# One transformer layer on one core: the feed-forward's next operands built two small steps per block instead of a pair of tiles at three places

## The chip, the cores and the metric

The kernel runs on one core of one Trainium2 chip. The metric is the time on the device in microseconds (us), a median over runs. A profile is one execution, taken by the hardware profiler. The engines are TensorE (PE; its weight loads are PEld), VectorE (DVE), ScalarE (ACT), GpSimd (POOL) and SyncE (SP). All DMAs of this kernel are issued from SP's queue, in the order in which they stand there.

## The reference, cut to what matters

One layer over 2048 latent tokens and 128 context tokens of width 1024: attention and a short convolution, an output projection, then a feed-forward network of hidden width 2816. The change lies in the feed-forward part, which works on all 2176 tokens:

```python
x = x + gate_a * rms_norm(mix, g_attn_post)
u = rms_norm(x, g_ffn_pre) * (1.0 + scale_f) + shift_f
gu = u @ w_ffn_in
h = jax.nn.silu(gu[..., :D_FF]) * gu[..., D_FF:]
return x + gate_f * rms_norm(h @ w_ffn_out, g_ffn_post)
```

Everything is float32.

## The kernel before, in words

**Stages.** Input projections, attention with the convolution and the output projection interleaved, then the feed-forward's up-projection (`u @ w_ffn_in`), then its down-projection. After the output projection each of the 17 tiles of 128 tokens (0 to 15 latent, 16 context) lies in DRAM as `x2d[ti]`, with its inverse norm in a column of `r2s`.

**Precision.** A float32 matrix is split into a high part, a cast by ScalarE (line 82), and the remainder, a subtraction by VectorE (line 83); `split` does both. A product is then three matmuls: high times high, high times low, low times high.

**The up-projection** uses Strassen's scheme in Winograd's form: the four quadrants of the weights of one block and the four quadrants of the operand `u` give seven combinations each, and seven products instead of eight. Columns of weights come in `NF` = 22 blocks (index `f`), tokens in three chunks (index `c`) of 5, 6 and 6 tiles. Two tiles form a pair: their quadrants b11 and b21 come from the first tile, b12 and b22 from the second. A single tile (the fifth of chunk 0) is halved instead. The matmuls are 320 columns wide in chunk 0 and 384 in chunks 1 and 2.

**One block** (`up_unit`, lines 948 to 992) is 7 products x 4 slices x 3 matmuls = 84 matmuls, lines 956, 957 and 959, into four PSUM banks called a, b, c and d (two buffers each, so all of PSUM). VectorE and ScalarE combine the banks (lines 965 to 984), POOL multiplies the second hidden half (line 986), and SP stores both halves. Beside it `wi_ops` (line 913) makes the next block's seven weight operands: POOL forms four sums `st` (line 918), then come seven splits into `wi`. The raw weights come by two loads of 512 KB a block, into the tag `t4`, which has four buffers.

**Building the operand.** The seven combinations of `u` for a pair of tiles come from `build_pair`, which calls `build_tile` for each tile: load the row `x2d[ti]` (512 KB, again a buffer of `t4`), scale it on POOL (line 835), then twice: four transposes on TensorE into one PSUM bank (line 841) and four scalings by VectorE into `ur` (line 842). Then come seven outputs; four of them need a subtraction on POOL first (line 859, tile `td`, two buffers). Chunk 0's are kept in SBUF (`build_kept`, during the output projections). Those of chunks 1 and 2 are built while the chunk before runs (`build_spilled`): each output is split into `hl`, which has one buffer, and stored to DRAM (512 KB to `u2d`). Their transposes use bank d. The operands come back by `u_load` from block 19 on.

**Order.** The program is written as one sequence, and each engine gets its own queue, drawn up when the program is built (`schedule_with_timeline_sim=True`): of what is ready on a simulated timeline, what was written earlier goes first. An engine then executes its queue in that order. So instructions of a build, written after block 2, stand among those of blocks 3 to 6 in each queue.

## Time and profile before

| | us |
|---|---|
| median of 3 runs | 3112.84 |
| lowest and highest | 3108.48, 3118.28 |
| the profiled execution | 3102.96 |
| its span, first to last instruction | 3101.2 |
| up-projection: first and last matmul start | 1570.7, 2574.5 |

The span is counted on the engines; the execution's time has a little more around it. Busy shares of the span: PE 94%, PEld 86%, DVE 67%, ACT 44%, POOL 42%. In the rows below, `L82` is line 82 of the kernel before; `out<-in` gives the tiles written and read; `x48` is a count; a bracket at a row's end holds the idle time of the engine before that instruction, and what ended it. Rows of one line and one tile give the shortest, median and longest duration in ns, then the first and last start in us. Rows of waits give the total in us, the number of times and the longest. Matmul ends are modelled by the profiler, so stretches of time are taken from one matmul's start to another's.

### The profile page before, as it was taken

The page shows a single profiled execution, that of the slowest core. Times are in us where ns is not written, and L with a number is a line of the kernel's source. Part 1 is how long each engine was busy: PE and PEld are TensorE (multiplying, and loading weights), DVE is VectorE, ACT ScalarE, POOL GpSimd, SP SyncE. Part 2 cuts the span into 40 slices and gives each one's busy share as a digit, 9 for nine tenths or more (in the row PEclk, how much of TensorE's full clock was granted, in tenths as well). Part 3 has the DMA queues.
Part 4 walks back from the last instruction along what each step waited for, and adds up shares of the span by engine and source line. Part 5 has one row for each costly group of instructions (what it writes and reads, how often), then busy time and mean ns, then how long its engine had stood idle before and what let it go on. Part 6 is the DMA issues. An engine that isn't in the chain of part 4 may idle for free.

```text
span 3101.2 us, 47350 instructions
## 1 busy us (share of the span) xinstructions
PE 2926.7 (94%) x16921; PEld 2661.2 (86%) x16921; DVE 2080.6 (67%) x4116; ACT 1370.9 (44%) x2425; POOL 1296.4 (42%) x1135
## 2 busy tenths in 40 slices
PE   4789989999999999999999999999999999999998
PEld 3567879999999999988888888999899998788886
DVE  7996547887887887764467775676655554554443
ACT  3433225665655665663444343333333333443333
POOL 7653115554554554542246554554544540111110
PEclk8899999999999999999999999999999999999999
DMA  6776473463464354347635565434643235666663
GB/s 248 234 227 218 154 244 112 120 213 107 120 191 125 109 177 129 110 152 228 203 129 161 154 192 192 155 129 147 216 156 101 96 103 187 237 227 217 219 217 121
DMA packets 351180, 525.26 MB, mean 169 GB/s; under 512 B 33088, under 2 KB 264672, under 8 KB 349152
## 3 DMA queue, kind: packets, MB, share of 16 engines
q1 hardware_dynamic: 350944, 522.23, 52.7%
q8 instruction: 133, 2.18, 0.3%
q14 instruction: 103, 0.84, 0.1%
HBM read 393.79 MB, written 128.34 MB: 168 GB/s over the span
## 4 chain that ended last, share of the span: by engine, by line
PE 65%; DVE 14%; DMA 8%; issue 7%; POOL 4%; ACT 2%; SPq 0%; POOLq 0%; DVEq 0%; ACTq 0%
PE psg L956 7%; PE psg L959 6%; PE psg L957 6%; PE s L502 6%; PE psy L1087 4%; PE psy L1085 4%; PE psy L1086 4%; PE t L546 3%; DVE wi L83 2%; DMA raw<-in_w_fi 2%; PE psx L725 2%; PE psx L726 2%; PE psx L724 2%; PE o L539 2%; DMA u2d<-hl 2%
## 5 line engine op out<-in xcount | busy, mean ns | idle before, releaser
L956 PE MATMUL psg<-u,wi 128*128 128x384 f32 (+1 forms) x1848 | 617.4, 335 | 42.6 <-ACT wi L82 18.0
L957 PE MATMUL psg<-u,wi 128*128 128x384 f32 (+1 forms) x1848 | 607.3, 329 | 0.0
L959 PE MATMUL psg<-u,wi 128*128 128x384 f32 (+1 forms) x1848 | 591.5, 331 | 4.5 <-DVE wi L83 4.5
L505 DVE TENSOR_SCALAR_CACHE_REDUCE e<-s 128x436 f32<-128x436 f32 (+2 forms) x648 | 373.4, 600 | 87.0 <-PE s L502 71.4
L956 PEld LDWEIGHTS psg<-u,wi 128*128 128x128 f32 x1848 | 351.6, 190 | 61.7 <-ACT wi L82 27.6
L959 PEld LDWEIGHTS psg<-u,wi 128*128 128x128 f32 x1848 | 348.5, 190 | 9.0 <-DVE wi L83 8.5
L502 PE MATMUL s<-km,qt 128*128 128x436 f32 (+1 forms) x1280 | 344.4, 372 | 10.8 <-DVE e L505 8.5
L957 PEld LDWEIGHTS psg<-u,wi 128*128 128x128 f32 x1848 | 352.0, 190 | 0.1
L83 DVE TENSOR_TENSOR wo<-rawo,wo 128x1024 fp32r<-128x1024 f32 x132 | 167.0, 1265 | 248.6 <-ACT wo L82 243.9
L83 DVE TENSOR_TENSOR wi<-st,wi 128x512 fp32r<-128x512 f32 x264 | 234.4, 892 | 131.3 <-ACT wi L82 129.7
L510 ACT ACTIVATE e<-e,nm 128x2176 f32<-128x2176 f32 (+1 forms) x136 | 273.9, 2014 | 76.9 <-DVE nm L509 76.2
L82 ACT CAST wi<-st 128x512 fp32r<-128x512 f32 x264 | 163.0, 620 | 324.1 <-POOL st L918 161.4
L1087 PE MATMUL psy<-wo,hhl 128*128 128x512 f32 x748 | 285.5, 390 | 1.8 <-DVE hhl L83 1.8
L1086 PE MATMUL psy<-wo,hhl 128*128 128x512 f32 x748 | 285.9, 390 | 0.9 <-DVE wo L83 0.9
L1085 PE MATMUL psy<-wo,hhl 128*128 128x512 f32 x748 | 285.6, 390 | 0.0
L82 ACT CAST wo<-rawo 128x1024 fp32r<-128x1024 f32 x132 | 139.1, 1054 | 297.7 <-PE psy L1087 288.6
L502 PEld LDWEIGHTS s<-km,qt 128*128 128x128 f32 x1280 | 209.4, 190 | 23.6 <-DVE e L505 16.3
L83 DVE TENSOR_TENSOR atl<-t,ath 128x512 fp32r<-128x512 f32 (+2 forms) x292 | 187.2, 650 | 34.2 <-ACT ath L82 33.6
L82 ACT CAST ath<-t 128x512 fp32r<-128x512 f32 (+2 forms) x292 | 157.3, 555 | 113.6 <-PE t L546 111.1
L1058 POOL TENSOR_TENSOR rr<-rr,mhalf 128x1 f32<-128x1 f32 x17 | 13.1, 779 | 450.2 <-DVE rr L1057 450.2
L918 POOL TENSOR_TENSOR st<-raw,st 128x512 f32<-128x512 f32 x66 | 103.4, 1566 | 229.7 <-DVE wi L83 229.7
L238 PE MATMUL pq<-wh,uh 128*128 128x512 f32 x408 | 172.4, 433 | 19.9 <-DVE t L297 15.2
(264 smaller groups left out, 7183.9 us busy)
## 6 DMA issues: line engine op xcount, KB each, us to landing
raw<-in_w_fi SPq DMA_DIRECT2D x132, 512.0 KB, 4.1
rawo<-in_w_fo SPq DMA_DIRECT2D x132, 512.0 KB, 3.5
fu<-ud SPq DMA_DIRECT2D x256, 256.0 KB, 4.7
raw<-in_w_ada SPq DMA_DIRECT2D x48, 512.0 KB, 4.8
u2d<-hl SPq DMA_DIRECT2D x42, 512.0 KB, 3.8
u<-u2d SPq DMA_DIRECT2D x14, 1536.0 KB, 9.5
hr<-hid SPq DMA_DIRECT2D x110, 192.0 KB, 3.5
hid<-hid SPq DMA_DIRECT2D x88, 192.0 KB, 1.9
```

What stands on the lines that cost most here:

```text
L82: S.copy(h, src)
L83: (eng or V).tensor_tensor(l, src, h.bitcast(F32), op=ALU.subtract)
L238: T.matmul(pq, u[kt][0][:, sl], wh[j, kt], start=(kt == 0), stop=False)
L502: mm = T.matmul(ps[:, :n], qt[:, s, m, t * P:(t + 1) * P], km[m][:, k0:k0 + n], start=(s == 0), stop=(s == 1))
L505: V.tensor_scalar(et[:, k0:k0 + n], ps[:, :n], SCALE, None, op0=ALU.mult, op1=ALU.max, accum_out=mx[:, ci:ci + 1])
L510: S.activation(et[:, :nk], et[:, :nk], AF.Exp, bias=nm, scale=1.0, accum_out=sm[:, t, m:m + 1])
L956: T.matmul(ps[:, :n], h[:, ks], u[:, 0, kt, :n], start=start and kt == 0, stop=False, skip_group_check=not start)
L957: T.matmul(ps[:, :n], h[:, ks], u[:, 1, kt, :n], start=False, stop=False, skip_group_check=not start)
L959: T.matmul(ps[:, :n], l[:, ks], u[:, 0, kt, :n], start=False, stop=stop and kt == 3, skip_group_check=not start)
L1085: T.matmul(banks[i][:, b, :], hh, woh_[:, bs], start=(f == 0), stop=False)
L1086: T.matmul(banks[i][:, b, :], hh, wol_[:, bs], start=False, stop=False)
L1087: T.matmul(banks[i][:, b, :], hl, woh_[:, bs], start=False, stop=(f == NF - 1))
```

## The change

`build_tile` and `build_pair` become generators, cut into steps. A tile has two steps of four transposes and four scalings (the first also has the row's load and its scaling on POOL); each of the seven outputs is a step, with its subtraction where it has one. A pair is 11 steps, a chunk 33. Before, a whole pair was written after blocks 2, 8 and 14 of the chunk that runs; now one step is written after block 0 and two after each of blocks 1 to 18, so that the 33 end with block 16. The outputs come in the order 2, 1, 3, 4, 0, 5, 6 instead of 0, 5, 6, 2, 1, 3, 4, for chunk 0's kept operands also. Nothing else differs: the same instructions on the same tiles and buffers.

```diff
@@ build_tile
+            yield ur
-        return ur
@@ build_pair
+        us = []
+        for ti in pair:
+            for ur in build_tile(ti, bank):
+                yield
+            us.append(ur)
         if len(pair) == 2:
-            ua, ub_ = (build_tile(ti, bank) for ti in pair)
+            ua, ub_ = us
...
-        out(0, w, b11)
-        out(5, w, b21)
-        out(6, w, b22)
         t = diff(b12, b11)
         out(2, w, t)
+        yield
         t2_ = diff(b22, t)
         out(1, w, t2_)
+        yield
         out(3, w, diff(t2_, b21))
+        yield
         out(4, w, diff(b22, b12))
+        yield
+        for i, src in ((0, b11), (5, b21), (6, b22)):
+            out(i, w, src)
+            yield
@@ build_kept
-        build_pair(chunks[0][k], pst_bank, out)
+        for _ in build_pair(chunks[0][k], pst_bank, out):
+            pass
@@ build_spilled
-    def build_spilled(c, k):
+    def build_spilled(c):
+        for i in range(7):
+            u2d[c, i] = dram.tile([P, 2, 4, widths[c]], F32, name=f"u2d{c}{i}")
+        for k, pair in enumerate(chunks[c]):
...
+            yield from build_pair(pair, lambda: bank("d"), out)
@@ for c in range(3): for f in range(NF):
-            if c < 2 and f % 6 == 2 and f // 6 < 3:
...
-                build_spilled(c + 1, f // 6)
+            if c < 2 and f < NF - 3:
+                steps = build_spilled(c + 1) if f == 0 else steps
+                for _ in range(2 if f else 1):
+                    next(steps, None)
```

## The prediction, made before the changed kernel ran

> **What bounds the kernel now.** I read the page first, then the feed-forward stage block by block. The page gives TensorE nearly the whole span and the largest share of the chain that ended last; the last row here is the stage that the change touches.

> ```profile
> span 3101.2 us, 47350 instructions
> PE 2926.7 (94%) x16921; PEld 2661.2 (86%) x16921; DVE 2080.6 (67%) x4116; ACT 1370.9 (44%) x2425; POOL 1296.4 (42%) x1135
> PE 65%; DVE 14%; DMA 8%; issue 7%; POOL 4%; ACT 2%; SPq 0%; POOLq 0%; DVEq 0%; ACTq 0%
> ...
> L956 PE MATMUL psg<-u,wi x1848: 302/334/657, 1570.7 to 2574.2; 128*128 128x384 f32 x125, 128*128 128x320 f32 x60
> ```

> The change lies in the up-projection, from 1570.7 us on, three chunks of 22 blocks. A block is 84 matmuls of lines 956 to 959 (seven products of four triples), so every 84th of them in the timeline marks a block's start. The busy times by stretch follow; after the two times stand its length, the engines' busy times, the granted clock, DMA share and GB/s. First chunk 0 without its first block and chunk 1 without its first two, then an undisturbed block of each width (320 and 384 columns).

> ```profile
> 1589.54:1890.39 300.85, 280.86 (x1813) 270.42 (x1813) 233.18 (x342) 122.39 (x232) 181.47 (x127) 0.98 0.51 155
> 1928.07:2251.44 323.37, 307.60 (x1730) 297.84 (x1730) 224.08 (x334) 121.16 (x224) 169.92 (x120) 0.99 0.50 163
> 1676.48:1688.80 12.32, 12.32 (x87) 12.32 (x85) 9.74 (x14) 5.08 (x10) 8.13 (x7) 1.00 0.54 151
> 2338.92:2353.48 14.56, 14.56 (x86) 14.56 (x86) 8.27 (x13) 5.35 (x10) 7.20 (x5) 1.00 0.31 101
> ```

> Undisturbed, a block is all TensorE. 21 blocks of 12.32 are 258.7 us, so chunk 0 has 42.1 us too much; 20 of 14.56 are 291.2, so chunk 1 has 32.2. Chunk 2, where nothing is built, has none. These **74.3 us** go with the six pairs built after blocks 2, 8 and 14. Rows of three kinds of build block: the one after the call (transposes, one store), the third (two stores), and two examples of the fourth, where the last three stores bunch. Chunk 0's six come first, then chunk 1's six, then the fourth blocks.

> ```profile
> 1615.07:1629.97 14.90, 13.71 (x94) 13.17 (x93) 11.91 (x25) 6.21 (x12) 4.99 (x4) 1.00 0.42 123
> 1701.30:1715.90 14.60, 13.84 (x94) 13.09 (x93) 10.42 (x21) 5.34 (x10) 4.60 (x5) 1.00 0.47 141
> 1790.94:1805.74 14.80, 13.94 (x95) 13.09 (x93) 10.60 (x21) 5.34 (x10) 4.41 (x5) 1.00 0.53 150
> 1644.97:1659.46 14.49, 13.12 (x87) 12.33 (x86) 14.46 (x17) 6.50 (x12) 10.77 (x8) 1.00 0.66 196
> 1731.21:1746.28 15.07, 13.45 (x87) 12.42 (x86) 13.16 (x17) 6.98 (x13) 10.53 (x7) 1.00 0.48 151
> 1820.72:1835.33 14.61, 13.19 (x87) 12.42 (x86) 12.74 (x16) 6.95 (x13) 10.54 (x7) 1.00 0.51 156
> 1943.50:1960.05 16.55, 15.95 (x95) 15.31 (x93) 9.39 (x20) 4.89 (x9) 4.76 (x5) 1.00 0.32 109
> 2039.49:2055.37 15.88, 15.60 (x92) 15.13 (x92) 9.87 (x19) 5.53 (x10) 4.66 (x4) 1.00 0.30 96
> 2134.80:2150.66 15.86, 15.58 (x92) 15.11 (x92) 9.87 (x19) 5.53 (x10) 4.61 (x4) 1.00 0.28 93
> 1976.27:1990.92 14.65, 14.65 (x86) 14.65 (x85) 12.20 (x15) 6.30 (x13) 9.26 (x7) 1.00 0.63 194
> 2072.50:2087.17 14.67, 14.67 (x86) 14.67 (x85) 12.00 (x15) 6.16 (x12) 9.11 (x8) 1.00 0.61 193
> 2168.43:2183.97 15.54, 15.00 (x86) 14.65 (x86) 11.80 (x17) 6.70 (x13) 9.77 (x7) 1.00 0.44 149
> 1659.46:1676.48 17.02, 14.10 (x87) 13.84 (x85) 13.13 (x17) 6.73 (x13) 10.57 (x8) 0.90 0.51 147
> 1990.92:2010.22 19.30, 16.89 (x85) 15.83 (x85) 14.35 (x18) 7.43 (x15) 12.43 (x9) 0.91 0.58 166
> ```

> The worst blocks are the fourth ones: 4.70 and 4.74 us over, at a granted clock of 0.90. The timeline at the end of the first of them shows why, and the waits of ScalarE in chunk 0, then chunk 1, show how often.

> ```profile
> 1666.01 0.62 ACT L82 CAST hl<-td 128x512 fp32r<-128x512 f32 x1 [5.48 <-DMA u2d<-hl]
> 1666.66 0.69 DVE L83 TENSOR_TENSOR hl<-td,hl 128x512 fp32r<-128x512 f32 x1 [3.53 <-ACT hl L82]
> 1667.27 0.48 DVE L975 TENSOR_TENSOR c<-psg,u 128x320 f32<-128x320 f32 x1
> 1667.81 0.41 PE L956 MATMUL psg<-u,wi 128*128 128x320 f32 x1 [2.92 <-DVE c L975]
> ...
> ACT hl L82 <- DMA u2d<-hl: 27.4, 10, 5.5
> ...
> ACT hl L82 <- DMA u2d<-hl: 21.2, 8, 4.7
> ```

> The staging tile `hl` has one buffer, so a cast waits until the store before it has landed. It stands in ScalarE's queue ahead of the weight casts, VectorE's split waits behind it, the sum behind that split, and TensorE for the sum's bank.

> **The change part by part.** Counts stay the same: per pair 2 row loads and 7 stores on SP, 2 row scalings and 4 subtractions on POOL, 16 transposes, 16 scalings and 7 splits on VectorE, 7 casts on ScalarE. The durations of these and of what they meet:

> ```profile
> L842 DVE TENSOR_SCALAR ur<-psg,modc x96: 394/402/413, 1615.5 to 2171.5; 128x128 f32<-128x128 f32 x96
> L83 DVE TENSOR_TENSOR hl<-td,hl x24: 679/1166/1783, 1653.1 to 2203.6; 128x512 fp32r<-128x512 f32 x24
> L859 POOL TENSOR_TENSOR td<-ur x12: 1272/1633/2277, 1636.7 to 2188.9; 128x512 f32<-128x512 f32 x12
> L835 POOL TENSOR_SCALAR row<-row,r2s x12: 1119/1391/1838, 1607.1 to 2126.6; 128x1024 f32<-128x1024 f32 x12
> DMA to landing us min/median/max: 3.5/3.8/9.1
> ```

> (1) *Spreading.* A pair was four blocks' work (3 to 6); now its 11 steps take 5.5, four with transposes (two blocks) and seven with stores (three and a half); 33 steps end in block 16, and the operands are first reloaded in block 19. VectorE gets 16 x 0.402 + 7 x 1.166 = 14.6 us per pair, 2.7 a block; POOL 2 x 1.391 + 4 x 1.633 = 9.3, 1.7 a block. What a block with two steps takes is in the rows above: the block after the call had 7 or 8 transposes, as now, and a store besides; the third had two stores, as now. No block has three.

> Chunk 1: the first kind averages 16.10 (1.54 over), the third 14.95 (0.39 over). Per pair 2 x 1.54 + 3.5 x 0.39 = 4.4, three pairs 13.3 against 32.2: **18.9 gained**. Its ends: nothing left but the transposes, 0.15 each ((15.86 - 14.56 - 0.28 idle) / 7), 7.2 for 48, which gains 25; or third blocks like 15.54 throughout, 3 x (3.1 + 3.4) = 19.5, which gains 12.7.

> Chunk 0: the same rows average 14.77 (2.45 over) and 14.72 (2.40 over), 3 x (4.9 + 8.4) = 39.9 of 42.1: only 2 gained at the low end. But those third blocks inherit the backlog of the two before (VectorE 14.46 of 14.49 us busy), and chunk 1's rows show the cost without one. At chunk 1's excess 28.8 would go. I stay nearer chunk 0's own rows, two parts to one: 2.15 and 1.73 over, 3 x (4.3 + 6.05) = 31, **11 gained**.

> (2) *Raw weights.* Row loads share the four buffers of the raw weights; POOL's wait for late raws in chunk 1, and the same row in chunk 2:

> ```profile
> L918 POOL TENSOR_TENSOR st<-raw 128x512 f32<-128x512 f32 x23 | 31.2, 1355 | 35.6 <-DMA raw<-in_w_fi 33.6 <-DVE wi L83 2.1
> L918 POOL TENSOR_TENSOR st<-raw 128x512 f32<-128x512 f32 x21 | 26.9, 1283 | 1.8 <-DMA raw<-in_w_fi 1.8
> ```

> Now one row is held at a time, across up to one block boundary, where two were. I count no gain apart: it is inside the proxies. Moved past on SP are raw loads and hidden-state stores; on POOL the weight sums. With an early or late row the bound is a step's wait of one landing, 3.8 us either way, per chunk start, where building now begins in block 0 instead of 2. Chunk 1's first block is late anyway, so I take 0.

> (3) *Order of the seven*: subtractions now lead, so a store's cast can wait for a subtraction (1.6 us); POOL has 4 to 5 us a block idle to hide it. Without that cover, 12 a chunk at 1.6 would cost up to 19 on VectorE's queue; the other end is a gain from first stores not waiting, under 1.

> (4) *The kept operands* of chunk 0 take the new order too, beside the output projections, where TensorE is full:

> ```profile
> 1530.00:1570.00 40.00, 40.00 (x180) 33.03 (x179) 15.88 (x26) 14.90 (x36) 7.93 (x11) 1.00 0.54 169
> ...
> L83 DVE TENSOR_TENSOR u<-td,u x12: 413/688/1562, 1457.7 to 1544.3; 128x512 fp32r<-128x512 f32 x8, 128x256 fp32r<-128x256 f32 x4
> ```

> The projections hide it: the last split starts at 1544.3, 26 us before the first block. I take 0, or with that cover gone 4 subtractions, 6.5 us.

> Sum: 18.9 + 11 = **30 us off** 3102.96 (the profiled execution, 1.8 over its span): 3073. The median shown, 3112.84, is 9.9 above that execution; against it, 3083.

> **Rivals.** *A, VectorE and POOL bind chunk 0.* VectorE is busy 9.74 of 12.32 us in its undisturbed block; with 2.7 more it is 12.4 of about 12.8, and each wait counts. For it: splits last 0.679 to 1.783 us, the longest as if they had waited out a subtraction (1.272). If such work always took turns, POOL's 7.20 us of an undisturbed block and 1.7 more, and 7 + 7 / 5.5 = 8.3 splits of 0.679 (5.6), would make 14.5 us a block, what chunk 0's build blocks show, and 16.5 blocks of that are 36 over: 6 gained, where the rows' own low end was 2. Against: the mean build split of 1.166 us, so turns are taken in part only. At the rows' 2 the total is 21: 3092. [...]

> *B, nothing is spread.* The engines' queues already stretched a pair over four blocks; 5.5 blocks instead of four may only move the same waits about. For it: the seconds of two stores must still wait for a landing of 3.8 us plus split and cast. Against: third blocks of 14.65. Time: 3113.

> *C, slower: the second cast.* Each block with two stores holds a cast that can block ScalarE, and the chain above then reaches TensorE. If each cost what the fourth blocks show (4.72 on average), three per pair and 18 in all are 85, with the transposes (14.4) 99 against 74.3: 25 slower, 3138. It decides above (74.3 - 14.4) / 18 = 3.3 us per such block. The rows have 0.09 to 0.98 in chunk 1, 2.2 to 2.8 in chunk 0, so chunk 0 alone comes near it.

> *D, smooth throughout.* Chunk 1 gains 25 and chunk 0 28.8, together 54: 3059.

> **How the numbers follow.** My forecast 0.44, A 0.20, B 0.14, C 0.12, D 0.10. The measurement tells 0.3%, 9.3 us here. Faster: forecast, A, D, 0.74; same: B, 0.14; slower: C, 0.12. The time is the forecast's. Leaving out C and a little of D, the range runs from 3058 to 3114. Within the forecast alone, the ends of chunk 0 (2 to 28.8) and chunk 1 (12.7 to 25) give 3059 to 3098.

> **What would show it.** In the changed profile: chunk 1 blocks of 14.6 to 16.1 us and none near 19; chunk 0 blocks of 13.5 to 14.8 up to block 16 and 12.3 after; the clock at 1.00 there; ScalarE's waits for the store no longer above 4 us, if not fewer; POOL's wait for raw weights in chunk 1 well under 33.6. The forecast is wrong if chunk 0's blocks all stand at 14.5 or more (A), if the two excesses still sum to about 74 (B), or if each block with two stores has a TensorE gap of 2 to 4 us behind a cast (C).

## The result, and the profile after

The forecast was wrong in sign. The changed kernel takes 3125.07 us (median of 10 runs, 3119.24 to 3127.34) against 3108.17 for the kernel before in the same rounds: a ratio of **1.0046**, 95% interval 1.0034 to 1.0057. Its profiled execution took 3120.22 us, 17.3 more than the one shown before.

The page after, same rows as before. Line numbers are nine higher from `wi_ops` on: the up-projection's matmuls are now L965, L966 and L968, the weight sums L927. The subtractions, which stand ahead of it, are L863.

```profile
span 3118.4 us, 47333 instructions
PE 2933.0 (94%) x16921; PEld 2667.5 (86%) x16921; DVE 2073.0 (66%) x4116; ACT 1370.5 (44%) x2425; POOL 1289.4 (41%) x1135
PE 64%; DVE 12%; DMA 9%; issue 7%; POOL 5%; ACT 2%; SPq 0%; POOLq 0%; DVEq 0%; ACTq 0%
```

The work is the same; the DMA's and POOL's shares of the chain rose by a point each. Now busy times by stretch: from the first block of chunk 0 to the first of chunk 2 (before, then after), then after's counterparts of the two stretches that the prediction began with, three blocks in a row of chunk 0 and the worst of chunk 1's build blocks.

```profile
1570.68:2251.44 680.76, 635.61 (x3793) 612.58 (x3794) 487.65 (x717) 264.89 (x494) 374.27 (x262) 0.98 0.51 166
```

```profile
1572.93:2268.13 695.20, 640.16 (x3794) 616.00 (x3793) 479.62 (x717) 264.69 (x494) 367.56 (x262) 0.97 0.50 162
1592.43:1902.95 310.52, 284.24 (x1814) 272.18 (x1813) 231.04 (x342) 122.12 (x232) 175.97 (x127) 0.97 0.49 150
1944.41:2268.13 323.72, 306.00 (x1724) 297.34 (x1723) 216.04 (x328) 121.54 (x224) 165.86 (x118) 0.99 0.50 161
1638.32:1655.42 17.10, 14.98 (x85) 13.96 (x86) 13.14 (x17) 7.22 (x14) 11.72 (x9) 0.90 0.42 133
1655.42:1672.43 17.01, 14.57 (x86) 13.78 (x85) 14.14 (x19) 7.04 (x13) 11.22 (x8) 0.90 0.58 170
1672.43:1689.53 17.10, 14.47 (x87) 13.93 (x86) 9.24 (x16) 6.10 (x12) 6.83 (x6) 0.90 0.62 172
2108.78:2128.91 20.13, 17.17 (x89) 16.48 (x89) 9.22 (x17) 4.92 (x9) 6.78 (x6) 0.92 0.33 101
```

The two chunks grew by 14.4 us (695.20 - 680.76): TensorE sat idle 9.9 us more (55.0 against 45.2) and was busy 4.5 us longer, at a granted clock of 0.97 against 0.98. Of the span's other 2.8 us, 2.3 come before the first block of the up-projection; that start lies anywhere from 1570 to 1581 us in the profiles of the kernels below, so these say little. Chunk 0's excess went from 42.1 to 51.8 us (310.52 less 258.7), chunk 1's from 32.2 to 32.5 (323.72 less 291.2), and chunk 1's first two blocks from 8.6 to 12.3. Four blocks of chunk 0 took 17.0 to 18.5 us, three of them in a row (shown), where 13.5 to 14.8 was forecast, and chunk 1 has one of 20.13 where none near 19 was.

The waits of ScalarE and POOL over both build chunks, before and then after (total us, times, longest):

```profile
ACT hl L82 <- DMA u2d<-hl: 48.6, 18, 5.5
...
POOL st L918 <- DMA raw<-in_w_fi: 45.3, 12, 8.0
```

```profile
ACT hl L82 <- DMA u2d<-hl: 59.6, 23, 4.8
...
ACT hl L82 <- POOL td L863: 13.4, 9, 4.2
...
POOL st L927 <- DMA raw<-in_w_fi: 89.7, 21, 16.7
```

Each of the three went the wrong way: casts wait for a store's landing 23 times instead of 18, for a subtraction 9 times where they never had, and POOL waits twice as long for raw weights. One place in the timeline after shows the whole chain, at the end of the third of those blocks:

```profile
1679.18 0.62 ACT L82 CAST hl<-ur 128x512 fp32r<-128x512 f32 x1 [3.64 <-DMA u2d<-hl]
...
1679.70 0.61 ACT L82 CAST wi<-raw 128x512 fp32r<-128x512 f32 x1
...
1679.83 0.69 DVE L83 TENSOR_TENSOR hl<-ur,hl 128x512 fp32r<-128x512 f32 x1 [3.40 <-ACT hl L82]
...
1680.37 0.42 PE L965 MATMUL psg<-u,wi 128*128 128x320 f32 x1 [2.49 <-ACT wi L82]
```

ScalarE stands 3.64 us before a build's cast; the weight cast queued behind it follows at once, and TensorE, idle for 2.49 us, starts on its result.

### The profile page after: what moved, and what is told of

It is laid out like the page before. It is cut to its first block, busy times and chain, and to the rows that moved or that the text cites. A ratio compares the mean times of both kernels' runs of the same rounds, so it can differ in the third digit from the quotient of the medians.

```text
span 3118.4 us, 47333 instructions
## 1 busy us (share of the span) xinstructions
PE 2933.0 (94%) x16921; PEld 2667.5 (86%) x16921; DVE 2073.0 (66%) x4116; ACT 1370.5 (44%) x2425; POOL 1289.4 (41%) x1135
## 4 chain that ended last, share of the span: by engine, by line
PE 64%; DVE 12%; DMA 9%; issue 7%; POOL 5%; ACT 2%; SPq 0%; POOLq 0%; DVEq 0%; ACTq 0%
PE s L502 7%; PE psg L965 6%; PE psg L968 6%; PE psg L966 6%; PE psy L1099 4%; PE psy L1097 4%; PE psy L1098 4%; DMA u2d<-hl 3%; PE t L546 3%; DMA raw<-in_w_fi 3%; POOL st L927 2%; PE pq L239 2%; DVE wi L83 2%; PE pq L240 2%; PE pq L238 2%
## 5 line engine op out<-in xcount | busy, mean ns | idle before, releaser
L965 PE MATMUL psg<-u,wi 128*128 128x384 f32 (+1 forms) x1848 | 618.1, 335 | 44.4 <-ACT wi L82 24.0
L966 PE MATMUL psg<-u,wi 128*128 128x384 f32 (+1 forms) x1848 | 609.3, 330 | 0.0
L968 PE MATMUL psg<-u,wi 128*128 128x384 f32 (+1 forms) x1848 | 594.3, 332 | 9.3 <-DVE wi L83 9.0
L965 PEld LDWEIGHTS psg<-u,wi 128*128 128x128 f32 x1848 | 353.1, 191 | 61.2 <-ACT wi L82 34.7
L968 PEld LDWEIGHTS psg<-u,wi 128*128 128x128 f32 x1848 | 349.7, 191 | 15.4 <-DVE wi L83 14.6
L966 PEld LDWEIGHTS psg<-u,wi 128*128 128x128 f32 x1848 | 353.4, 191 | 0.2
L83 DVE TENSOR_TENSOR wo<-rawo,wo 128x1024 fp32r<-128x1024 f32 x132 | 167.0, 1265 | 249.1 <-ACT wo L82 244.3
L83 DVE TENSOR_TENSOR wi<-st,wi 128x512 fp32r<-128x512 f32 x264 | 239.9, 911 | 132.4 <-ACT wi L82 130.4
L82 ACT CAST wi<-st 128x512 fp32r<-128x512 f32 x264 | 162.8, 620 | 324.6 <-POOL st L927 165.7
L82 ACT CAST wo<-rawo 128x1024 fp32r<-128x1024 f32 x132 | 139.1, 1054 | 298.4 <-PE psy L1099 289.2
L83 DVE TENSOR_TENSOR atl<-t,ath 128x512 fp32r<-128x512 f32 (+2 forms) x292 | 187.1, 650 | 33.6 <-ACT ath L82 33.1
L82 ACT CAST ath<-t 128x512 fp32r<-128x512 f32 (+2 forms) x292 | 157.2, 554 | 114.5 <-PE t L546 112.4
L927 POOL TENSOR_TENSOR st<-raw,st 128x512 f32<-128x512 f32 x66 | 102.6, 1555 | 216.4 <-DVE wi L83 216.3
L238 PE MATMUL pq<-wh,uh 128*128 128x512 f32 x408 | 172.6, 434 | 16.3 <-DVE t L297 12.7
```

The costliest lines, as they stand in the source:

```text
L82: S.copy(h, src)
L83: (eng or V).tensor_tensor(l, src, h.bitcast(F32), op=ALU.subtract)
L238: T.matmul(pq, u[kt][0][:, sl], wh[j, kt], start=(kt == 0), stop=False)
L965: T.matmul(ps[:, :n], h[:, ks], u[:, 0, kt, :n], start=start and kt == 0, stop=False, skip_group_check=not start)
L966: T.matmul(ps[:, :n], h[:, ks], u[:, 1, kt, :n], start=False, stop=False, skip_group_check=not start)
L968: T.matmul(ps[:, :n], l[:, ks], u[:, 0, kt, :n], start=False, stop=stop and kt == 3, skip_group_check=not start)
```

## The experiments

All runs, each against the kernel before in its own rounds. "Chunks 0+1" is the profiled time from the first block of chunk 0 to the first of chunk 2 (every 84th matmul), before 680.8. This column is one execution each, up to 7 us off its run's median time: e1's is the slowest of its 12, e7's and e10's the fastest of theirs, and the one before about 5 us faster than its median. e1 to e4 shared one chip and its runs of the kernel before, as did e5 to e8, e9 to e12 and f1 to f4.

| run | edit | ratio, 95% interval | chunks 0+1, us |
|---|---|---|---|
| after | the change | 1.0046, 1.0034 to 1.0057 | 695.2 |
| e1 | change, two `hl` | 1.0025, 1.0015 to 1.0035 | 694.0 |
| e2 | change, one own row buffer | 1.0003, 0.9994 to 1.0012 | 687.0 |
| e3 | change, both | 1.0000, 0.9991 to 1.0009 | 680.6 |
| e4 | change, old order | 1.0029, 1.0020 to 1.0038 | 690.8 |
| e5 | before, one own row buffer | 1.0099, 1.0083 to 1.0115 | 714.5 |
| e6 | before, one own row buffer, two `hl` | 1.0086, 1.0070 to 1.0102 | 706.9 |
| e7 | stores tied to blocks, one own row buffer | 0.9942, 0.9927 to 0.9957 | 661.6 |
| e8 | stores tied to blocks | 0.9970, 0.9958 to 0.9982 | 676.3 |
| e9 | before, two own row buffers | 0.9971, 0.9960 to 0.9981 | 672.9 |
| e10 | change, two own row buffers | 1.0032, 1.0021 to 1.0044 | 684.9 |
| e11 | e7, old order, last stores drawn out | 0.9908, 0.9894 to 0.9922 | 653.2 |
| e12 | e11, two row buffers | **0.9901, 0.9885 to 0.9916** | 649.0 |
| f1 | e10 with the old order | 0.9983, 0.9974 to 0.9992 | 677.3 |
| f2 | f1, first step after block 2 | 0.9956, 0.9944 to 0.9969 | 665.0 |
| f3 | before with only the new order | 1.0034, 1.0021 to 1.0046 | 692.1 |
| f4 | f3, two own row buffers | 1.0048, 1.0034 to 1.0062 | 688.8 |

### What the waits name: the staging tile, the rows, the order (e1 to e4)

The edits, on the changed kernel; e3 is e1 and e2 together:

```diff
# e1
-tag="hl", name="hl", bufs=1
+tag="hl", name="hl", bufs=2
# e2
-row = t4("row")
+row = t4("row") if bank is pst_bank else bld.tile([P, D], F32, tag="rowb", name="row", bufs=1)
# e4: the loop over outputs 0, 5, 6 stands ahead of the first subtraction
+for i, src in ((0, b11), (5, b21), (6, b22)):
+    out(i, w, src)
+    yield
 t = diff(b12, b11)
```

> The changed kernel with two staging buffers hl instead of one; nothing else. Theory S (store cycle): two stores in each of 3.5 blocks per pair keep the single buffer's cycle of cast, split and landing (5.5 to 7 us) running without a break, ScalarE waits in it for 59.6 us in all (23 times), and that is where the time went; with two buffers these waits fall under 10 us and the kernel gains 20 us or more: ratio to before 0.995 to 0.998. Theory R (rows): the loss comes from raw weights that land late because a row holds one of their four buffers; ratio stays at 1.003 to 1.005. Theory L (load): VectorE and POOL bind chunk 0 without any pause between pairs; ratio 1.002 to 1.005.

> The changed kernel with one buffer of their own for the rows of the spilled builds, so that the four raw buffers hold raw weights alone; nothing else. Theory R: POOL's and ScalarE's waits for raw weights in chunks 0 and 1 fall to what chunk 2 has, a few us, and the kernel gains 10 us or more: ratio to before 0.996 to 1.001. Theory S and theory L: ratio 1.003 to 1.005, since the waits for raws end work that waits for the store or for VectorE anyway.

> Both buffers added to the changed kernel. If S and R are each real and separate, the gains add: ratio 0.985 to 0.993. If both are real but cover each other, the ratio is near the better of the two alone. Theory L: no better than 1.000, with chunk 0's blocks 1 to 17 still at 14 us or more.

> The changed kernel with the seven outputs in the old order (0, 5, 6, then 2, 1, 3, 4), still two steps per block. Theory O (order): with a subtraction in front, the first store of a pair waits for all four transposing steps and for POOL, and the last three come back to back; the old order takes that back and gains 5 to 10 us, ratio 1.001 to 1.003. Theory S: the cycle of the single buffer is the same in either order, ratio 1.003 to 1.006.

Each edit took something back: the row buffer most (0.43%, 13 us), the second `hl` 0.2%, the old order 0.17%; e3 stands level with the kernel before and no better (the intervals of e1 and e4 just overlap the change's). So the theories of the rows and of the order came out within their ranges (e2, e4), that of the store cycle did not (e1 was to reach 0.998), and the gains don't add (e3). The waits of e2, then of e1:

```profile
ACT hl L82 <- DMA u2d<-hl: 67.5, 29, 5.1
...
POOL st L927 <- DMA raw<-in_w_fi: 12.2, 2, 6.1
```

```profile
ACT hl L82 <- DMA u2d<-hl: 24.5, 14, 4.8
ACT hl L82 <- POOL td L863: 21.8, 15, 4.5
```

With its own buffer for rows, POOL's wait for raw weights falls from 89.7 to 12.2 us: in the change it was rows held in the weights' four buffers that made the weights late. The casts then wait more for landings (67.5), as if late weights had kept the stores apart in part. With two `hl`, the waits for landings more than halve, but casts wait for subtractions instead (21.8), and a pair's seven stores, from the first cast to the last landing, pack into 29 to 44 us in e3 where they took 47 to 65 in the change: a second buffer lets the queues draw the same burst closer, it doesn't spread it.

### The same parts in the kernel before (e5, e6, e9)

Row buffers are added to the kernel before, with e2's line (`bufs=1` in e5; with two `hl` as well in e6; `bufs=2` in e9).

> The kernel before with one buffer of their own for the rows of the spilled builds; nothing else. Theory R1: a row in a raw buffer costs whatever the steps are; in the kernel before POOL waits 45.3 us for raw weights, so this gains too: ratio to before 0.994 to 0.998. Theory R2: the blocks without any build between two pairs (12.3 and 14.6 us) took that loss up already, and only the changed kernel, which has none, shows it: ratio 0.999 to 1.001.

> The kernel before with the row's own buffer and two staging buffers hl. Theory S (the store's wait on ScalarE ends in TensorE's worst gaps, 4.7 us over in each fourth block): with two buffers another 10 us or more go, ratio 0.990 to 0.995. Rival P (packing): the queues are drawn up greedily, so a second buffer only lets the stores of a pair follow one another faster, the load of two blocks comes in one and a half, and nothing is gained over the row's buffer alone: ratio within 0.001 of that kernel's.

> The kernel before with two buffers of their own for the rows of the spilled builds. With one (an earlier run) the second row of a pair was loaded only when the first was transposed, and TensorE waited up to 7 us for POOL's scaling of it; with two that wait is gone. Theory R1 (a row in a raw buffer costs the kernel before too): ratio to before 0.994 to 0.998. Theory R2 (its blocks without builds absorb it): 0.999 to 1.001. Rival K (the shared buffers hold the build back, and without them the whole pair runs in a burst): 1.002 to 1.006.

One buffer costs the kernel before 1%, which neither theory had expected, and two gain it 0.3%; the second `hl` of e6 takes back 0.13%, within the noise. A whole pair written in one place wants both rows at once: with one buffer the second row's load waits for the first tile's transposes, and TensorE, whose queue already holds the second tile's, waits for POOL's scaling of that row, once per pair (e5):

```profile
PE psg L841 <- POOL row L835: 31.5, 6, 7.0
```

With two, TensorE has no such wait, and POOL's wait for raw weights falls from 45.3 to 13.7 us:

```profile
POOL st L918 <- DMA raw<-in_w_fi: 13.7, 2, 6.9
```

So rows in the weights' buffers cost the kernel before some 9 us too, and a comparison of the change with spare buffers against the kernel before without them would credit the change with what the buffers bring.

### Making the stores really spread (e7, e8, e11, e12)

Nothing in the change ties a step to its block: an engine's queue takes what is ready. To see what is in the queues, the casts into `hl` in ScalarE's queue are placed here by the number of blocks begun ahead of them (copies of line 965, now 974, one per block), for the three pairs built in chunk 0:

```
before  4 5 5 6 6 6 7     10 11 11 12 12 12 13    16 17 17 18 18 19 19
after   4 5 5 5 6 6 6     10 10 11 11 11 12 12    15 16 16 16 17 17 18
e7      5 5 6 6 7 9 10    10 11 11 12 14 15 15    15 16 16 16 17 17 18
e11     4 5 6 6 7 9 10    10 11 11 12 14 15 15    15 16 16 17 18 19 19
```

The change has a pair's seven stores in three blocks, or four for the last pair, with three stores in some of them; before, they stood in four. In e7 and e8 an output's step is issued only behind a weight cast of the block that it is meant for; transposes are written in blocks 1, 2, 6, 7, 11 and 12, and `ur` has four buffers for them.

```diff
 def split(h, l, src):
-    S.copy(h, src)
+    cast = S.copy(h, src).ins
...
+    return cast
 # wi_ops: an output listed for block f goes behind the weight cast of s2 or s3
+def step(cast):
+    for _ in range(OUTS.get((steps, cast[0]), 0) if steps is not None else 0):
+        with tc.issue_after(cast[1]):
+            next(todo_o.pop(0))
-split(*dst[1], s2)
+step((0, split(*dst[1], s2)))
-split(*dst[4], s3)
+step((1, split(*dst[4], s3)))
```

e7 has a row buffer, e8 has not. e11 is e7 with the old order and the last pair's stores out to block 20; e12 gives it two row buffers and three of `ur`.

> The changed kernel with the rows' own buffer, and the seven stores of a pair truly spread: each store's cast is put behind a named weight cast of a later block in ScalarE's queue, about one a block (in the queue they stand in blocks 5, 5, 6, 6, 7, 9, 10 for the first pair, where the changed kernel has 4, 5, 5, 5, 6, 6, 6); four buffers ur instead of two, so that the next pair's transposes need not wait for the last stores. Theory B (the change never spread the stores, and a spread that reaches them pays): the excess of the two chunks falls from some 88 us in the kernel with the rows' buffer to 50 or 60, ratio 0.988 to 0.993. Theory L (VectorE and POOL bind chunk 0 whatever the order): chunk 0's blocks 2 to 17 stay near 14.4 us, ratio 0.997 to 1.001.

> The same spread of the stores and the same four buffers ur, but the rows take raw buffers as in the kernels before and after. It separates the spread from the rows. If the rows alone made the change slower and the spread of stores pays by itself: ratio 0.994 to 0.999, 10 to 25 us better than the changed kernel. If the two only pay together: 1.002 to 1.005.

> The spread kernel with the rows' own buffer, and now also the old order of the outputs and the last pair's stores drawn out to block 20 (the products 0 and 1, reloaded first, come early in that order), so that the last seven stores no longer share four blocks. Theory B: in the spread kernel the last pairs have the waits for the store that are left (up to 4.75 us on ScalarE); without them ratio 0.990 to 0.993. If the load of chunk 0 is what is left: 0.993 to 0.996, the same as the spread kernel.

> The same with two buffers for the rows and three for ur instead of one and four. TensorE's waits for POOL's scaling of a row (3.1 us in the spread kernel) should go: 0.001 better than with one row buffer, if three ur do not hold the next pair's transposes; else 0.001 to 0.003 worse.

The tied kernels gain: e8 0.3% with rows still in the weights' buffers, e7 0.58% (theory B had asked for 0.7% or more), e11 and e12 0.92% and 0.99%. But e8 differs from the change in three things at once: the ties, the blocks in which the transposes are written, and four `ur` instead of two. No run takes these apart, nor the two edits that part e11 from e7, so what the ties give by themselves is not shown. The waits of e12 (the split's cast is line 84 there) and its stretch:

```profile
ACT hl L84 <- DMA u2d<-hl: 12.6, 7, 3.6
```

```profile
1580.19:2229.23 649.04, 619.55 (x3792) 603.65 (x3793) 489.65 (x717) 262.00 (x494) 369.34 (x262) 0.99 0.53 173
```

A quarter of the waits for a landing is left, TensorE's idle time is 29.5 us instead of 45.2, and VectorE is as busy as before (489.65 us against 487.65). A pair's stores take 60 to 97 us, against 54 to 64 before. e12 beats both kernels, and with the same two row buffers in the kernel before (e9) still by 0.7%, 23.9 us in the two chunks.

### What the order, the rows and the start cost by themselves (e10, f1 to f4)

The question left open was the order of the seven outputs, which the prediction had set to nothing. f3 puts it alone into the kernel before; f4 and e10 add two row buffers to f3 and to the change; f1 is e10 with e4's order. f2 also moves the start:

```diff
# f3: the kernel before
-out(0, w, b11)
-out(5, w, b21)
-out(6, w, b22)
 t = diff(b12, b11)
...
 out(4, w, diff(b22, b12))
+out(0, w, b11)
+out(5, w, b21)
+out(6, w, b22)
# f2: f1 with
-if c < 2 and f < NF - 3:
-    steps = build_spilled(c + 1) if f == 0 else steps
-    for _ in range(2 if f else 1):
+if c < 2 and 2 <= f < NF - 3:
+    steps = build_spilled(c + 1) if f == 2 else steps
+    for _ in range(2):
```

> The changed kernel with two buffers of their own for the rows instead of one. With one, POOL waited 17 us for rows and the kernel stood at 1.0003. If that wait still cost something: 0.997 to 0.999. If the stores' bunching is all that is left: 0.999 to 1.001.

> The changed kernel with the old order of the outputs and two buffers for the rows. Theory O (the order and the rows make up the whole loss): as fast as the kernel before with two row buffers, ratio 0.996 to 0.998. Theory D (drawing the transposes out costs by itself, since no block is left without building): 1.000 to 1.002.

> The same, with the first step after block 2 instead of block 0, two steps a block to block 18. Theory E (early start: the first blocks of a chunk are late anyway, and steps there delay the catching up): 2 to 5 us better than without the shift, 0.001 to 0.002 in the ratio. If the start does not matter: within 0.001.

> The kernel before with the new order of the outputs alone, whole pairs at three places, rows in the raw buffers. Theory O: the first stores can no longer go while the second tile is transposed, which costs 4 to 8 us, ratio 1.0015 to 1.003. Theory D: the order does not matter, 0.999 to 1.001.

> The kernel before with the new order and two buffers for the rows. Theory O: 0.9985 to 1.001, worse by 0.0015 to 0.004 than the old order with the same buffers (0.9971). Theory D: 0.996 to 0.998.

**Order.** Alone it costs 0.34%, 11.3 us in the two chunks: three quarters of the change's whole loss. With two row buffers it costs 0.77% in the kernel before (e9 to f4) and 0.49% in the change (f1 to e10). The stores of the first pair show how, before and then in f3 (count: shortest, median, longest ns, first and last start):

```profile
L82 ACT CAST hl<-td x4: 612/618/620, 1652.3 to 1671.7; 128x512 fp32r<-128x512 f32 x4
...
L82 ACT CAST hl<-ur x3: 616/621/623, 1624.6 to 1644.3; 128x512 fp32r<-128x512 f32 x3
```

```profile
L82 ACT CAST hl<-td x4: 604/622/626, 1641.0 to 1663.3; 128x512 fp32r<-128x512 f32 x4
...
L82 ACT CAST hl<-ur x3: 617/619/619, 1670.2 to 1683.5; 128x512 fp32r<-128x512 f32 x3
```

Outputs 0 and 5 need only the first tile, and none of the three needs a subtraction. In the old order they went out from 1624.6 on, beside the second tile's transposes, 20 us for three casts. In the new order no cast can start before the second tile is there, 16.4 us later (13.6 counted from each run's own first block), and the seven follow in one chain through the one `hl`: a pair's stores take 51 us from first cast to last landing in f3 (mean of six pairs) against 59 before. The waits of f3, to be set beside the 48.6 above (with two row buffers the waits for a landing go from 50.2 us in e9 to 69.1 in f4):

```profile
ACT hl L82 <- DMA u2d<-hl: 64.3, 24, 4.5
...
ACT hl L82 <- POOL td L859: 22.8, 11, 5.6
```

**Rows.** Own buffers are worth 0.29% to the kernel before (e9), 0.28% to the tied spread (e8 to e7), and 0.43% (one) or 0.14% (two, within the noise) to the change. Why two help the change less than one isn't settled; e10's casts wait longer for landings (79.8 us against 67.5), but the profiled executions of e10 and e2 don't show the difference at all (684.9 and 687.0 us in the two chunks).

**Start.** The change's first step follows block 0 of a chunk. From f1 to f2 (start after block 2, the same order and buffers) the ratio goes from 0.9983 to 0.9956, with intervals that don't overlap: 0.27%, 8 us. In the profiles the first three blocks of the two chunks take 107.0 us together in f1 and 97.3 in f2, most of the 12.3 us between their chunks. The expectations had these costs too small: f2, f3 and f4 all moved further than the theory that names their cause had said, f1 just missed theory O's range, and e10 came out worse than both of its theories.

With all three mended, the steps as the change writes them give 0.9956 (f2), where the kernel before with the same row buffers gives 0.9971 (e9). The intervals overlap: that two small steps per block, by themselves, gain anything is not shown.

## Why the prediction was wrong

**The bottleneck was read rightly, the remedy not priced against it.** The chain quoted ahead of the change (store, cast into `hl`, weight cast, sum, TensorE) stands in the build blocks after, too, and e12 has less of it. TensorE's waits for a weight cast in both chunks, before, after and in e9:

```profile
PE psg L956 <- ACT wi L82: 18.0, 15, 3.7
...
PE psg L965 <- ACT wi L82: 24.0, 22, 2.5
...
PE psg L956 <- ACT wi L82: 7.8, 9, 3.0
```

Not all of it is the store's: in e9 these waits fall to 7.8 us with the casts' waits for a landing as long as before (50.2 us), so late raw weights end there too. The prediction then let the change shorten that chain without asking whether two stores a block fit the one buffer.

**Step (1), the spreading, failed in its proxy.** It was to bring 30 us. With the order, the rows' buffers and the start put right (f2), the small steps are 0.15%, 4.7 us, ahead of whole pairs with the same row buffers (e9), which is not clear of noise. "What a block with two steps takes is in the rows above" put two stores at the third block's 0.39 us over (chunk 1) and 1.73 (chunk 0). The casts of chunk 1's first pair in the kernel before, ScalarE's queue in the timeline:

```profile
1978.26 0.62 ACT L82 CAST hl<-ur 128x512 fp32r<-128x512 f32 x1 [1.66 <-DVE ur L842]
1984.59 0.61 ACT L82 CAST hl<-td 128x512 fp32r<-128x512 f32 x1
...
1998.82 0.62 ACT L82 CAST hl<-td 128x512 fp32r<-128x512 f32 x1 [4.69 <-DMA u2d<-hl]
2003.73 0.62 ACT L82 CAST hl<-td 128x512 fp32r<-128x512 f32 x1 [1.55 <-DMA u2d<-hl]
```

That block (1976.27 to 1990.92) held the third and fourth stores, whose casts found the buffer free, because the old order had let two go early; the sixth and seventh waited for landings. In the change a store's round is a cast of 0.62 us, a split of 0.7 to 1.8 and a landing of 3.5 to 5 (median 3.9, the longest 12.9), mostly 5 to 7 us, and two fill most of a block of 12.3 or 14.6. "No block has three" was wrong as well, by the queues above. The backlog that was to excuse chunk 0's third blocks was read from one of its three rows (VectorE 14.46 of 14.49 us; the others have 13.16 of 15.07 and 12.74 of 14.61).

By rival C's own sum, the excess of 84.3 us (51.8 + 32.5) less 14.4 for transposes is 3.9 us for each of its 18 blocks: above its point of decision (3.3) and below its price (4.72). So C, at 0.12, has the number nearest to what came (25 us slower forecast, 16.9 measured), but not by its mechanism: it asked for a gap of 2 to 4 us behind a cast in each such block, and after has two such gaps (2.49 and 2.37 us). What grew is the number of shorter ones: TensorE has 24 gaps of over 1 us in the two chunks, where it had 10.

**Step (2), raw weights at 0, was mis-sized and of the wrong sign.** "One row is held at a time, across up to one block boundary" is not what the queues did. In all six pairs the second row's load starts while the first row is still waiting for its transposes, 17 to 26 us ahead of the last of them; of the first pair, the load of the second row, then the first row's last transposes:

```profile
1600.05 0.43 SPq L75 DMA_DIRECT2D row<-x2d  x1
...
1618.89 0.38 PE L841 MATMUL psg<-ident,row 128*128 128x128 f32 x2
```

A row holds its buffer from its load to its last transposes, 41.9 us on average, some three blocks, against 36.1 before. POOL's wait in chunk 1, forecast "well under 33.6":

```profile
POOL st L927 <- DMA raw<-in_w_fi: 57.2, 10, 16.7
```

The bound given, one landing per chunk start, left out that a held row takes one of four buffers from loads that come twice a block. What this cost the change is less than the 13 us that e2 takes back, since such rows cost the kernel before 9 (e9): the difference is some 4 us, an estimate, as e2 has one row buffer and e9 two.

**Step (3), the order at 0 between -1 and 19, was mis-sized, by a cost that it doesn't name.** By ratio it costs 10 us alone (f3) and about 24 with two row buffers (f4 against e9). The parts don't add up: put back into the change, the old order regains 5 us while rows still hold weights up (e4), and 15 where they don't (e10 to f1). The prediction looked for a cost in the subtraction's wait alone (13.4 us of ScalarE's in the profile after; its bound of 19 is one chunk's 12 subtractions, both chunks have 24, or 38 us), and of the first stores it said only that they might gain "under 1". That was the error: what the old order gave was stores that started while the second tile was being transposed.

**Early start**, named only as a possible landing's wait, cost 8 us in f1 against f2. **Step (4)**, the kept operands, at 0, is borne out as far as the starts above can show it: those of the two orders overlap (1570.4 to 1581.1 us with the old, 1570.1 to 1579.0 with the new).

**The rivals.** A's floor of 14.5 us a block in chunk 0 isn't one: VectorE is busy 231.04 of 310.52 us there, and e12 does the same work in blocks 2 to 17 at 13.8 us on average. But chunk 0 keeps 27.2 us of excess in e12, against 12.3 in chunk 1, and e7's same blocks average 14.3, so a part of A may hold; no run settles it. B (nothing is spread) is right about the stores, whose waits only moved about, but it had them move at no cost. D (54 us off) is reached by no run: e12's two chunks are 31.7 us shorter than before, which happens to lie near the forecast's 30, but 7.9 of them are what the row buffers bring without any steps (e9).

## What to carry to other kernels

Cutting work into small steps doesn't spread it when the engines' queues are drawn up by readiness and the steps share one staging buffer: count the rounds of that buffer (cast, split, landing) that a block must hold, and look in the queues for where the steps landed; the three fastest kernels here had theirs tied to their places. A reorder among independent outputs is a change of its own: ask of each what it needs first, and what early starters were filling. And a tile that borrows buffers from a prefetch is priced by how long it holds them as well, not only by how many are held at a time.

## What the runs showed of the hardware

The granted clock fell to 0.90 in blocks whose longest idle gap was under 3 us: 2.92 in the kernel before, 2.49 in the block of the chain after. The first of the three blocks shown (1638.32 to 1655.42, also 0.90) has no longer gap than this one, ahead of a build's transposes:

```profile
1640.22 0.47 PE L841 MATMUL psg<-ident,row 128*128 128x128 f32 x1 [1.34 <-DVE ur L842]
```

Inside each of these blocks the clock is at 1.00 but for one stretch of 3.41 us at 0.50. Here are the 3.41 us with the gap of 2.49 us and the stretch behind them; TensorE's busy time stands first, the clock after the five engines:

```profile
1677.65:1681.06 3.41, 0.79 (x4) 0.33 (x3) 1.24 (x3) 1.77 (x4) 1.00 (x1) 1.00 0.76 206
1681.06:1684.47 3.41, 3.41 (x13) 3.37 (x14) 3.41 (x7) 1.35 (x3) 0.81 (x1) 0.50 0.54 154
```

So such a block loses more than its gap: the one of the chain took 17.10 us, TensorE busy for 14.47 of them, with the work that an undisturbed block does in 12.32. In its timeline the matmuls start 0.147 us apart at 1.00 and 0.268 apart at 0.50, so the 3.41 us do the work of 1.9 (an estimate). There are 9 such stretches in the two chunks before and 11 after; e12's clock of 0.99 over 649.04 us leaves room for two to five. So of the 31.7 us between before and e12 some 6 to 11 are the clock's (an estimate, at 1.5 us a stretch), and come on top of the idle time that e12 saves.
